# Layer 1's feed-forward with seven block products per hidden tile instead of eight, on one core

## The chip, the core and the metric

The kernel runs on one core of one Trainium2 chip. The core has a matrix engine (PE in the profile, TensorE), three elementwise engines (DVE = VectorE, ACT = ScalarE, POOL = GpSimd), DMA queues that are fed by SP (SyncE), an on-chip memory SBUF of 128 partitions, and a small accumulator memory PSUM that the matrix engine writes. The metric is the device time of one execution in microseconds.

## The reference

A two-layer transformer block for 512 latent tokens and 256 context tokens of width 1024. Each layer is attention followed by a SwiGLU feed-forward, both behind a normalisation with a learned shift, scale and gate. Layer 0 treats latents and context, layer 1 (the last) gives only the latents. The part that the change touches is the feed-forward of layer 1, with F = 2816 hidden units:

```python
def _swiglu(h, w_in, w_out):
    gate, up = jnp.split(h @ w_in, 2, axis=-1)
    return (jax.nn.silu(gate) * up) @ w_out
...
x = x + gx2 * _swiglu(_rms(x, norm_ffn_w[l]) * (1.0 + scx2) + shx2, ffn_w_in[l], ffn_w_out[l])
```

Here `h` is 512 x 1024, `w_in` 1024 x 5632 (gate columns, then up columns), `w_out` 2816 x 1024, all float32; `gx2` is one row of 1024 numbers, the gate row.

## The kernel before

**Split products.** The large products are made in float32r. Every float32 operand z is split in two: `hi` is z rounded to float32r by an ACT copy, `lo = z - hi` is a subtraction (DVE or POOL). A product is three matmuls, hi·hi, hi·lo and lo·hi, accumulated in PSUM. `unit` (L322) loads a raw weight tile by DMA into one of two "raw" buffers (`raw_tile`, L101), and splits it; its argument `sub` names who subtracts. `by_pieces` (L314) subtracts by POOL in pieces of 256 columns.

**Operands.** `hT` holds the normalised activations transposed, hi and lo, each 128 x 8 x 512: partition = place within one of eight groups of 128 inputs, then group k, then token.

**The feed-forward** `ffn` (L786). The 2816 hidden units are 22 F-tiles of 128, taken in 11 pairs p. For a pair, gate and up weights come as four raw tiles of 128 x 4 x 256 (two halves of the inputs, 256 hidden units each), the down weights as two tiles of 128 x 1024. For each F-tile, `half` (L807) makes gate and up with 8 groups x 3 matmuls each, all 512 tokens at once in layer 1, into one PSUM tile `pgu` (two of these exist, tag "sc"). Then ACT makes silu(gate) (L841), DVE multiplies by up (L843), and `split` makes the hidden tile's hi and lo (L444, L445). The down product then sums over the F-tiles at hand (two; the last four together) for each of 4 token tiles x 2 halves of the output columns in one of four PSUM banks (`dps`, L868 to L870), and `residual` (L435) multiplies by the gate row `g` (L438) and adds into the token tile `xs[t]` (L439), both on DVE. `g` is made by `gate_row` (L248), which goes through DRAM, in the first pair. The first pair of layer 1 is made in two halves of 256 tokens, since the second half's `hT` is ready later. When the last sums of a half row are done, that half row goes to `out`.

**Ahead of it**, layer 1's attention runs over 8 heads. `in_proj1` (L607) loads four weight units for a head (two groups of inputs each, 128 x 768), split by ACT and, all four, by POOL in pieces. The output projection has eight weight units (`units1`, L1114): those with k = 4 to 7 live in the pool "w1u", which afterwards holds gate and up weights. Unit k = 6 has a raw tile of its own (`late_raw`), the others use the two shared raw buffers.

**What sets the order.** The framework schedules each engine's instructions from a simulated timeline, by program order as priority and by when operands are ready there; each engine then works off its list strictly in that order. A buffer of a ring is written again only after its last reader. A pool that is opened on the place of a closed one waits tile by tile for what lay there.

## Time and profile before

| | |
|---|---|
| median of three runs | 1791.71 us (1789.78 to 1797.6) |
| profiled execution | 1790.93 us, its span 1789.1 us |
| PE busy | 1718.5 us, 96% of the span |
| DVE, ACT, POOL busy | 998.0, 807.0, 608.9 us |
| mean granted PE clock | 0.992 of full |
| feed-forward of layer 1 | from 1411.2 us to the end |

PE's busy time holds overlaps of pipelined matmuls, so it doesn't show how densely PE works; the distance in time between starts of neighbouring matmuls does. "PEld" is the weight load of a matmul, which overlaps the one before. In a table of stages the columns are the stretch, its length, the busy time of each engine with the number of instructions in brackets, the granted clock, the DMA engines' busy share, and GB/s. In a timeline the columns are start, duration, engine, line, operation, output<-inputs and shape, and in square brackets how long the engine had been idle and who ended that.

### The profile page before, as it was taken

The numbers are of one execution on the slowest core, as the hardware profiler recorded it, in microseconds if no ns is written. First come the engines' busy times: TensorE is split into PE (matmuls) and PEld (weight loads), VectorE is DVE, ScalarE is ACT, GpSimd is POOL, SyncE is SP. The second block draws the span as 40 slices with busy tenths as digits, with TensorE's granted clock in tenths as the row PEclk, the third lists the DMA queues.
The fourth block names the chain that finished last, engine by engine and source line by source line (L and its number), as shares of the span: only waits on it lengthen the run. The fifth ranks groups of instructions, "written<-read, shape, count | busy, mean of one in ns | idle before, by whom it ended". The sixth has DMA issues, their size and how long they took to land.

```text
span 1789.1 us, 26195 instructions
## 1 busy us (share of the span) xinstructions
PE 1718.5 (96%) x9958; PEld 1455.3 (81%) x9958; DVE 998.0 (56%) x1738; ACT 807.0 (45%) x1713; POOL 608.9 (34%) x880
## 2 busy tenths in 40 slices
PE   6999999989999999999999999999988999999998
PEld 4987776767888888888888889999976888888887
DVE  4776465435265555555552756666564565656653
ACT  6666555434264344343332566666653432232230
POOL 2753333321054344222231767777752200000000
PEclk8999999999999999999999999999999999999999
DMA  9112233203552334343331211111121243233231
GB/s 318 53 42 88 79 100 124 72 31 112 161 156 80 100 104 152 122 130 126 109 97 45 85 36 47 44 49 41 57 71 60 69 131 96 71 114 98 71 111 54
DMA packets 152478, 165.64 MB, mean 93 GB/s; under 512 B 16481, under 2 KB 139937, under 8 KB 152353
## 3 DMA queue, kind: packets, MB, share of 16 engines
q1 hardware_dynamic: 152000, 163.77, 29.5%
q8 instruction: 78, 1.28, 0.3%
q14 instruction: 48, 0.39, 0.1%
q10 hardware_dynamic: 352, 0.21, 0.0%
HBM read 159.73 MB, written 4.22 MB: 92 GB/s over the span
## 4 chain that ended last, share of the span: by engine, by line
PE 71%; issue 6%; POOL 6%; ACT 4%; DVE 4%; DMA 4%; SPq 1%; ACTq 0%; POOLq 0%; DVEq 0%
PE pgu L813 13%; PE pu L813 8%; PE pg L813 8%; PE dps L868 5%; PE dps L869 5%; PE dps L870 5%; PE inps L431 3%; PE inps L432 3%; PE inps L433 3%; POOL wil L320 2%; PE av L582 2%; PE sc L537 2%; PE ops L752 2%; PE ops L754 2%; PE ops L753 2%
## 5 line engine op out<-in xcount | busy, mean ns | idle before, releaser
L438 DVE TENSOR_TENSOR dps<-dps,g 128x512 f32<-128x512 f32 x200 | 136.0, 695 | 105.2 <-PE dps L870 96.8
L868 PE MATMUL dps<-wdh,hdh 128*128 128x512 f32 x440 | 175.9, 401 | 1.7 <-DVE x L439 1.0
L869 PE MATMUL dps<-wdl,hdh 128*128 128x512 f32 x440 | 174.4, 396 | 0.0
L870 PE MATMUL dps<-wdh,hdl 128*128 128x512 f32 x440 | 167.8, 396 | 0.0
L431 PE MATMUL inps<-wih,hT 128*128 128x384 f32 x384 | 132.9, 346 | 1.8 <-ACT qkv L629 1.1
L439 DVE TENSOR_TENSOR x<-x,dps 128x512 f32<-128x512 f32 x200 | 131.9, 681 | 2.6
L433 PE MATMUL inps<-wih,hT 128*128 128x384 f32 x384 | 130.8, 341 | 0.0
L432 PE MATMUL inps<-wil,hT 128*128 128x384 f32 x384 | 130.5, 340 | 0.0
L813 PE MATMUL pu<-hT,wuh 128*128 128x512 f32 x352 | 129.4, 391 | 0.5 <-DVE x L439 0.5
L813 PE MATMUL pg<-hT,wgh 128*128 128x512 f32 x352 | 129.8, 392 | 0.0
L212 ACT ACTIVATE modw<-modw,cols 128x256 f32<-128x256 f32 x192 | 82.1, 498 | 82.5 <-DMA modw<-in_mod_w_dram 78.2
L813 PE MATMUL pgu<-hT,wuh 128*128 128x512 f32 (+1 forms) x384 | 113.3, 376 | 0.0
L813 PE MATMUL pgu<-hT,wgh 128*128 128x512 f32 (+1 forms) x384 | 112.3, 376 | 0.4 <-DVE hT L308 0.4
L868 PEld LDWEIGHTS dps<-wdh,hdh 128*128 128x128 f32 x440 | 82.7, 188 | 23.6 <-issue 3.3
L813 PE MATMUL pg<-hTc,wgh 128*128 128x256 f32 x352 | 99.0, 285 | 2.7 <-ACT hTc L307 2.4
L333 ACT CAST wgh<-wgr 128x1024 fp32r<-128x1024 f32 x44 | 46.0, 1049 | 121.9 <-PE pgu L813 71.2
L813 PE MATMUL pu<-hTc,wuh 128*128 128x256 f32 x352 | 98.4, 284 | 0.0
L870 PEld LDWEIGHTS dps<-wdh,hdl 128*128 128x128 f32 x440 | 82.3, 188 | 19.6
L869 PEld LDWEIGHTS dps<-wdl,hdh 128*128 128x128 f32 x440 | 82.8, 188 | 17.8
L334 DVE TENSOR_TENSOR wgl<-wgr,wgh 128x1024 fp32r<-128x1024 f32 x44 | 55.0, 1254 | 75.3 <-ACT wgh L333 75.3
L320 POOL TENSOR_TENSOR wil<-wir,wih 128x256 fp32r<-128x256 f32 x96 | 76.4, 824 | 56.3 <-ACT wih L333 56.0
L334 DVE TENSOR_TENSOR wul<-wur,wuh 128x1024 fp32r<-128x1024 f32 x44 | 58.1, 1321 | 61.8 <-ACT wuh L333 61.8
(263 smaller groups left out, 4626.1 us busy)
## 6 DMA issues: line engine op xcount, KB each, us to landing
modw<-in_mod_w_dram SPq DMA_DIRECT2D x96, 512.0 KB, 4.5
wgr<-in_ffn_w_in_dram SPq DMA_DIRECT2D x44, 512.0 KB, 3.5
wur<-in_ffn_w_in_dram SPq DMA_DIRECT2D x44, 512.0 KB, 3.5
wdr<-in_ffn_w_out_dram SPq DMA_DIRECT2D x44, 512.0 KB, 3.5
wir<-in_od_w_in_dram SPq DMA_DIRECT2D x96, 128.0 KB, 2.3
x<-in_x_dram SPq DMA_DIRECT2D x8, 512.0 KB, 6.7
wir<-in_ev_w_in_dram SPq DMA_DIRECT2D x16, 256.0 KB, 2.9
wor<-in_ev_w_out_dram SPq DMA_DIRECT2D x8, 512.0 KB, 3.9
```

Source lines behind the costliest of these rows:

```text
L212: nc.scalar.activation(pr[:, k], w[:, k], AF.Copy, scale=cols[:, kk:kk + 1])
L320: nc.gpsimd.tensor_sub(lo[c], raw[c], hi[c])
L334: (sub or nc.vector.tensor_sub)(lo, raw, f32(hi))
L431: nc.tensor.matmul(ps, hs[0][:, k, :], a, start=k == 0, stop=False)
L432: nc.tensor.matmul(ps, hs[0][:, k, :], b, start=False, stop=False)
L433: nc.tensor.matmul(ps, hs[1][:, k, :], a, start=False, stop=k == KT - 1)
L438: nc.vector.tensor_mul(tmp, ps, g[:, n * 512:(n + 1) * 512])
L439: eng.tensor_add(xt[:, n * 512:(n + 1) * 512], xt[:, n * 512:(n + 1) * 512], tmp)
L813: nc.tensor.matmul(ps[:, s0:s1], a, cols_T(b, s0, s1)[:, k, :], start=k == 0 and q == 0, stop=k == KT - 1 and q == 2)
L868: nc.tensor.matmul(ps, hh, a, start=j == 0, stop=False)
L869: nc.tensor.matmul(ps, hh, b, start=False, stop=False)
L870: nc.tensor.matmul(ps, hl, a, start=False, stop=j == nj - 1)
```

## The change

Layer 1 no longer calls `ffn` but a new function, `ffn_by_blocks`; layer 0 keeps `ffn`. The first pair of F-tiles is made as before (in blocks, `plain_pair`). For each of the other 20 F-tiles, gate and up together are seen as a product of 2 x 2 blocks: weight rows gate and up, the inputs in two halves of 512, the tokens in two halves of 256. Eight block products would be needed in the plain way; here seven are made (Strassen's scheme in Winograd's form), each of 4 groups x 3 matmuls with 256 tokens.

- Weight sums, per F-tile: with a11, a12 the input halves of gate and a21, a22 those of up, r1 = a21+a22, r2 = r1-a11, a11-a21 and a12-r2, on POOL (`combine`), each 128 x 512. Seven weight blocks are split: ACT rounds, POOL subtracts for two of them, DVE for five. They live in a ring of nine (`wb`).
- Activation sums, once: `context` makes four sums t1 to t4 of `hT`'s quarters (128 x 4 x 256 each; three chains on DVE, one on POOL, in two shared raw buffers and two of the four "wr" buffers) and splits them.
- Sums of products, per F-tile: one ACT copy and seven DVE additions of 128 x 256 in PSUM, ahead of silu.
- Weights come as 128 x 8 x 128 tiles, one for gate and one for up per F-tile, in a ring of four ("wr").
- Down sums: x is written to `out` after the first pair, `xs[t]` becomes an accumulator that ACT fills from the first sums, and later sums are added by DVE without the gate row. After the sums of F-tiles 16 and 17 the gate row is made, x is read back, and `xs = xs * g + x`. The sums of the last four F-tiles go through `residual` as before.
- In the input projection, heads 0 and 1 have two of their four weight units subtracted by DVE instead of POOL. In the output projection, unit k = 6 uses the shared raw buffers. The pool "w1u" is closed ahead of the feed-forward, and pools for the blocks and the down weights are opened.

```diff
--- before.py
+++ after.py
@@ -613,7 +613,7 @@
                     yield raw[:, :, j * P:(j + 1) * P], od_w_in[
                         0, u * 256:(u + 1) * 256, j * D + h * P:j * D + (h + 1) * P].rearrange(
                         "(j p) n -> p j n", p=P)
-            ws.append(unit(wh, views, [P, 2, 384], 5, "wi", by_pieces))
+            ws.append(unit(wh, views, [P, 2, 384], 5, "wi", None if h < 2 and u % 2 else by_pieces))
         kT = st.tile([P, 2, TOK], F32R, name="kT", tag="kT")
         vv = st.tile([P, NT, P], F32, name="vv", tag="vv")
         qs = {}
@@ -872,6 +872,168 @@
                     if p == NF // 2 - 1:
                         done(t, n)
             wo, hid = [], []
+
+    def ffn_by_blocks(l, xs, new_blocks, new_down, fp, rooms, done):
+
+        half = KT // 2
+        cols = SEQ // 2
+        wf = ffn_w_in[l]
+        hh = [fp.tile([P, SEQ], F32R, name=f"hd{z}", tag=f"hd{z}", bufs=4) for z in "hl"]
+
+        def load(f, up):
+            raw = fp.tile([P, KT, P], F32, name="wr", tag="wr", bufs=4)
+            c0 = up * FFN + f * P
+            nc.sync.dma_start(raw, wf[:, c0:c0 + P].rearrange("(j p) n -> p j n", p=P))
+            return raw[:, :half], raw[:, half:]
+
+        def block():
+            return [new_blocks(z) for z in "hl"]
+
+        def halves(raw, eng=nc.vector):
+            hi, lo = block()
+            nc.scalar.copy(hi, raw)
+            eng.tensor_sub(lo, raw, f32(hi))
+            return hi, lo
+
+        def combine(a, b, op):
+            r = fp.tile([P, half, P], F32, name="ws", tag="ws", bufs=4)
+            nc.gpsimd.tensor_tensor(r, a, b, op)
+            return r
+
+        def down(f):
+            raw = raw_tile([P, D], "wdr")
+            hi, lo = new_down("h"), new_down("l")
+            nc.sync.dma_start(raw, ffn_w_out[l, f * P:(f + 1) * P, :])
+            nc.scalar.copy(hi, raw)
+            nc.vector.tensor_sub(lo, raw, f32(hi))
+            return hi, lo
+
+        def product(out, a, b, start=True, stop=True):
+            for k in range(half):
+                for x, y, q in ((a[0], b[0], 0), (a[0], b[1], 1), (a[1], b[0], 2)):
+                    nc.tensor.matmul(out, x[:, k, :], y[:, k, :], start=start and k == 0 and q == 0,
+                                     stop=stop and k == half - 1 and q == 2)
+
+        b11, b12, b21, b22 = ([hT[z][0][:, k * half:(k + 1) * half, c * cols:(c + 1) * cols] for z in range(2)]
+                              for k in range(2) for c in range(2))
+
+        def places():
+            ps = p_sc.tile([P, 1024], F32, name="pgu", tag="sc")
+            return ps, ps.rearrange("p (r c) -> p r c", c=cols)
+
+        def hidden(ps, first=None):
+            pu, pg = ps[:, :SEQ], ps[:, SEQ:]
+            sg = fp.tile([P, SEQ], F32, name="sg", tag="sg", bufs=1)
+            nc.scalar.activation(sg, pg, AF.Silu)
+            nc.vector.tensor_mul(pu, sg, pu)
+            hi, lo = first or [fp.tile([P, SEQ], F32R, name=f"hd{z}", tag=f"hd{z}", bufs=4) for z in "hl"]
+            nc.scalar.copy(hi, pu)
+            nc.vector.tensor_sub(lo, pu, f32(hi))
+            return hi, lo
+
+        def plain_pair():
+            ws, ps = [], []
+            for f in range(2):
+                raws = [load(f, up) for up in range(2)]
+                ws.append([[halves(r) for r in raw] for raw in raws])
+                ps.append(places())
+            for c, bs in enumerate(((b11, b21), (b12, b22))):
+                for f in range(2):
+                    for up in range(2):
+                        for k in range(2):
+                            product(ps[f][1][:, (0 if up else 2) + c], ws[f][up][k], bs[k], k == 0, k == 1)
+            return [hidden(ps[0][0], hh), hidden(ps[1][0])]
+
+        def context():
+            t1, t2, t3 = (room() for room in rooms)
+            sub, add = ALU.subtract, ALU.add
+            f1, f2 = (raw_tile([P, half, cols], f"tf{i}") for i in range(2))
+            f3, f4 = (fp.tile([P, half, cols], F32, name=f"tf{i}", tag="wr", bufs=4) for i in (2, 3))
+            for eng, t, terms in ((nc.vector, f1, ((b12[0], b11[0], sub), (None, b12[1], add), (None, b11[1], sub))),
+                                  (nc.gpsimd, f3, ((b22[0], b12[0], sub), (None, b22[1], add), (None, b12[1], sub))),
+                                  (nc.vector, f2, ((b22[0], f1, sub), (None, b22[1], add))),
+                                  (nc.vector, f4, ((b21[0], f2, sub), (None, b21[1], add)))):
+                for a, b, op in terms:
+                    eng.tensor_tensor(t, t if a is None else f32(a), f32(b), op)
+            for t, raw in ((t2, f2), (t1, f1), (t3, f3), (b12, f4)):
+                nc.scalar.copy(t[0], raw)
+                nc.vector.tensor_sub(t[1], raw, f32(t[0]))
+            return t1, t2, t3, b12
+
+        def by_blocks(f):
+            (a11, a12), (a21, a22) = (load(f, up) for up in range(2))
+            w11 = halves(a11)
+            r1 = combine(a21, a22, ALU.add)
+            r2 = combine(r1, a11, ALU.subtract)
+            s2 = halves(r2, nc.gpsimd)
+            s1 = halves(r1, nc.gpsimd)
+            s3 = halves(combine(a11, a21, ALU.subtract))
+            w12 = halves(a12)
+            s4 = halves(combine(a12, r2, ALU.subtract))
+            w22 = halves(a22)
+            ps, z = places()
+            e, b, a, c = (z[:, i] for i in range(4))
+            q, u, v, w = (fp.tile([P, cols], F32, name=n, tag=n, bufs=1) for n in "quvw")
+            product(a, w11, b11)
+            nc.scalar.copy(q, a)
+            product(b, s2, t2)
+            nc.vector.tensor_add(u, b, q)
+            product(c, s1, t1)
+            nc.vector.tensor_add(v, c, u)
+            product(e, s3, t3)
+            nc.vector.tensor_add(b, e, v)
+            nc.vector.tensor_add(w, e, u)
+            product(a, w12, b21)
+            nc.vector.tensor_add(a, a, q)
+            product(c, s4, b22)
+            nc.vector.tensor_add(c, c, v)
+            product(e, w22, t4)
+            nc.vector.tensor_add(e, e, w)
+            return hidden(ps)
+
+        def sums(hid, wd, last, first):
+            for t in range(NTX):
+                for n in range(2):
+                    turn["sum"] = (turn["sum"] + 1) % 4
+                    ps = p_1.tile([P, 512], F32, name="dps", tag=("acc0", "tr0", "acc1", "tr1")[turn["sum"]])
+                    for j in range(len(hid)):
+                        x, y = (z[:, t * P:(t + 1) * P] for z in hid[j])
+                        a, b = (z[:, n * 512:(n + 1) * 512] for z in wd[j])
+                        nc.tensor.matmul(ps, x, a, start=j == 0, stop=False)
+                        nc.tensor.matmul(ps, x, b, start=False, stop=False)
+                        nc.tensor.matmul(ps, y, a, start=False, stop=j == len(hid) - 1)
+                    acc = xs[t][:, n * 512:(n + 1) * 512]
+                    if first:
+                        nc.scalar.copy(acc, ps)
+                    elif last:
+                        residual(xs[t], ps, g, n)
+                        done(t, n)
+                    else:
+                        nc.vector.tensor_add(acc, acc, ps)
+
+        g = None
+        hid, wd = [], []
+        for f in range(0, NF, 2):
+            if f == 0:
+                hid.extend(plain_pair())
+                t1, t2, t3, t4 = context()
+                for t in range(NTX):
+                    nc.sync.dma_start(out[0, t * P:(t + 1) * P, :], xs[t])
+            else:
+                hid.extend([by_blocks(f), by_blocks(f + 1)])
+            wd.extend([down(f), down(f + 1)])
+            if f == NF - 4:
+                continue
+            if f == NF - 6:
+                g = gate_row(l, 5, 0, fp)
+            sums(hid, wd, f == NF - 2, f == 0)
+            if f == NF - 6:
+                for t in range(NTX):
+                    xr = raw_tile([P, D], "xr")
+                    nc.sync.dma_start(xr, out[0, t * P:(t + 1) * P, :])
+                    nc.vector.tensor_mul(xs[t], xs[t], g)
+                    nc.vector.tensor_add(xs[t], xs[t], xr)
+            hid, wd = [], []
 
     class Pairs:
 
@@ -1108,15 +1270,12 @@
     def out_pool(k):
         return woe.pool if k < 2 else in_ctx_room if k < 4 else w1[0].pool
 
-    def late_raw(shape, name):
-        return opa.pool.tile(shape, F32, name=name, tag="wor", bufs=1)
-
     def units1():
         subs = (by_pieces, by_pieces, by_pieces, by_pieces, None, nc.gpsimd.tensor_sub, None, nc.gpsimd.tensor_sub)
         for k in range(KT):
             def views(raw, k=k):
                 yield raw, od_w_out[0, k * P:(k + 1) * P, :]
-            yield unit(out_pool(k), views, [P, D], 2 if k < 2 else 4, "wo", subs[k], late_raw if k == 6 else raw_tile)
+            yield unit(out_pool(k), views, [P, D], 2 if k < 2 else 4, "wo", subs[k])
 
     oproj = OutProj(1, units1(), o_t, xs)
 
@@ -1171,14 +1330,27 @@
     states[0].close()
     at.close()
     woe.close()
-    w1.append(Pool("w1d", "right"))
+    w1.pop().close()
+    blocks = Pool("w1b", "right")
+    downs = Pool("w1d", "right")
     fp = Pool("ffn1")
-    ffn(1, xs, NTX, w1, fp.pool,
-        lambda t, n: nc.sync.dma_start(out[0, t * P:(t + 1) * P, n * 512:(n + 1) * 512],
-                                       xs[t][:, n * 512:(n + 1) * 512]))
+
+    def new_room(j):
+        if j < 2:
+            if not rooms:
+                rooms.extend(ctx_room([P, 2, KT // 2, SEQ // 2], F32R, "tc"))
+            return rooms[j][:, 0], rooms[j][:, 1]
+        return [keep.tile([P, KT // 2, SEQ // 2], F32R, name=f"t3{z}", tag="xo", bufs=6) for z in "hl"]
+
+    rooms = []
+    ffn_by_blocks(1, xs, lambda z: blocks.pool.tile([P, KT // 2, P], F32R, name="wb" + z, tag="wb" + z, bufs=9),
+                  lambda z: downs.pool.tile([P, D], F32R, name="wd" + z, tag="wd" + z, bufs=4), fp.pool,
+                  [lambda j=j: new_room(j) for j in range(3)],
+                  lambda t, n: nc.sync.dma_start(out[0, t * P:(t + 1) * P, n * 512:(n + 1) * 512],
+                                                 xs[t][:, n * 512:(n + 1) * 512]))
     fp.close()
-    w1[1].close()
-    w1[0].close()
+    downs.close()
+    blocks.close()
 
 
 def _constants():
```

## The prediction

> **What bounds the kernel now.** I read the stage table of the feed-forward first, then the groups of instructions in its even part, then single instructions. The stage table of the kernel before (PE's last block of the first pair ends at 1436.4, the last sum at 1784.6):
>
> ```profile
> core 0: us, PE busy (x) PEld busy (x) DVE busy (x) ACT busy (x) POOL busy (x), PEclk, DMA share, GB/s
> 1411.17:1436.40 25.23, 24.78 (x210) 24.36 (x208) 14.71 (x23) 15.01 (x24) 2.92 (x3) 1.00 0.45 142
> 1439.95:1761.90 321.95, 321.95 (x1381) 258.93 (x1380) 184.74 (x241) 80.58 (x96) 0.00 (x0) 1.00 0.31 93
> 1761.90:1784.61 22.71, 22.71 (x97) 17.91 (x96) 10.52 (x16) 1.19 (x2) 0.00 (x0) 1.00 0.20 78
> ...
> 1527.60:1729.00 201.40, 201.40 (x865) 161.99 (x864) 118.83 (x156) 50.80 (x60) 0.00 (x0) 1.00 0.32 94
> ```
>
> From 1440 on PE has no gap: 864 matmuls of 512 tokens in 201.40 us are one every 0.2331 us, at full clock, and a pair of F-tiles (96 for gate and up, 48 for down) takes 33.6. DVE works 59% of that stretch, ACT 25%, POOL and most of the DMA not at all. So here the number of columns that PE streams sets the time, and fewer columns shorten it until another engine or a late operand takes over. What follows prices both.
>
> **PE's part.** Plain: 48 matmuls of 512 tokens per F-tile. By blocks: 7 x 4 x 3 = 84 of 256, each with a weight load of its own. The old first pair has just that form:
>
> ```profile
> 1425.38:1436.12 10.74, 10.74 (x95) 10.74 (x93) 0.50 (x1) 0.60 (x1) 1.00 0.46 149
> L813 PEld LDWEIGHTS pgu<-hT,wuh x384: 187/187/192, 1417.0 to 1761.3; 128*128 128x128 f32 x192
> ```
>
> Of the 93 loads one was under way at the start: 92 matmuls in 10.74 us, 0.1167 each, so that the loads of 0.188 overlap and cost nothing. Saved per F-tile: 48 x 0.2331 - 84 x 0.1167 = 11.19 - 9.80 = 1.39 us, for 20 F-tiles **27.7**. The new pitch can't be much under half of the old (0.1155: 29.8 saved), and at 0.1245, with transposes in between, 14.6 would be left. The first pair keeps its columns, the down sums theirs, and the last sums (22.7 us, then 4.5 to the end) are the same: 0 each.
>
> **What the other engines get.** Means of one, from the even stretch and, for POOL and the 256-wide PSUM operation, from the whole run:
>
> ```profile
> L439 DVE TENSOR_TENSOR x<-x,dps 128x512 f32<-128x512 f32 x64 | 41.6, 680 | 0.3
> L334 DVE TENSOR_TENSOR wgl<-wgr,wgh 128x1024 fp32r<-128x1024 f32 x16 | 19.6, 1226 | 21.8 <-ACT wgh L333 21.8
> L843 DVE TENSOR_TENSOR pgu<-sg,pgu 128x512 f32<-128x512 f32 x16 | 11.1, 693 | 18.7 <-ACT sg L841 18.7
> L445 DVE TENSOR_TENSOR hdl<-pgu,hdh 128x512 fp32r<-128x512 f32 x16 | 10.9, 682 | 0.0
> L333 ACT CAST wgh<-wgr 128x1024 fp32r<-128x1024 f32 x16 | 16.8, 1050 | 63.3 <-PE pgu L813 63.3
> L444 ACT CAST hdh<-pgu 128x512 fp32r<-128x512 f32 x16 | 9.4, 584 | 6.1 <-DVE pgu L843 6.1
> L587 DVE TENSOR_TENSOR o<-av,o 128x256 f32<-128x256 f32 x24 | 10.1, 421 | 31.3 <-PE av L582 31.0
> L213 POOL TENSOR_TENSOR modw<-modw 128x512 f32<-128x512 f32 x48 | 62.1, 1294 | 83.5 <-ACT modw L212 83.5
> L334 POOL TENSOR_TENSOR wol<-wor,woh 128x1024 fp32r<-128x1024 f32 x10 | 24.5, 2456 | 18.6 <-ACT woh L333 18.6
> ```
>
> Per pair of F-tiles, against PE's new 2 x 9.80 + 48 x 0.2331 = 30.8 us:
> - DVE: per F-tile five splits of 0.68, one down split of 1.23, seven additions of 0.42, silu's product and the hidden split 1.38, together 9.0; and eight plain additions of 0.68 per pair where there were sixteen operations (the product with g is gone): 23.4.
> - POOL: 12 operations of 1.29: 15.5.
> - ACT: per F-tile eight casts or copies of 0.58 at most, a down cast of 1.05, silu and hidden cast 1.2: 13.9.
> - DMA: the same bytes per F-tile in 8% less time; a 512 KB tile lands in 3.5 us (last fence) of the 15.4 that an F-tile takes, three of them, and two F-tiles of raw weights are in flight.
>
> None reaches 30.8 by itself. But DVE and POOL now work on SBUF together, which the old feed-forward of layer 1 never did. Layer 0's shows what that costs:
>
> ```profile
> 520.79 1.29 POOL L213 TENSOR_TENSOR modw<-modw 128x512 f32<-128x512 f32 x1
> 521.45 1.73 DVE L334 TENSOR_TENSOR wul<-wur,wuh 128x1024 fp32r<-128x1024 f32 x1
> ...
> 628.30 1.62 DVE L334 TENSOR_TENSOR wul<-wur,wuh 128x1024 fp32r<-128x1024 f32 x1
> 628.80 1.72 POOL L215 TENSOR_TENSOR ma<-modw 128x256 f32<-128x256 f32 x1
> ...
> L334 DVE TENSOR_TENSOR wul<-wur,wuh 128x1024 fp32r<-128x1024 f32 x22 | 31.2, 1417 | 28.1 <-ACT wuh L333 28.1
> 418.00:960.00 542.00, 538.33 (x2932) 455.36 (x2931) 284.28 (x384) 217.60 (x393) 169.64 (x166) 1.00 0.38 120
> ```
>
> A split that starts 0.63 before POOL's operation ends takes 0.50 longer; whoever starts second waits. With POOL busy 31% of the time a split took 0.19 more (1.417 against 1.226). With POOL at 15.5 of 30.8, 50%, I take 0.31 for each of DVE's twelve two-input SBUF operations per pair: 3.7, so DVE at 27.1 of 30.8. The least is 0, the most a whole POOL operation each, 15.5, which makes 38.9. I take PE to stay the bound, with **3** us lost in all where an addition that PE waits for stands behind a blocked split (bounds 0 and, as a rival, below): the product sequence gives each of those additions two products, 2.8 us, before its place is written again.
>
> The Trainium skill, page "SBUF — State Buffer", section "Who interferes with whom", says that a DVE instruction with two SBUF inputs and a POOL instruction that reads SBUF exclude each other, and the second fully blocks until the first is done. The rows above agree (1.73 against 1.23). By its words alone every collision costs up to a whole instruction, which is the 38.9 above and the third rival below; by the mean row it is 27.1.
>
> **The start.** The four activation sums need all of `hT`:
>
> ```profile
> 1423.99 1.29 DVE L308 TENSOR_TENSOR hT<-nhc,hT 128x512 fp32r<-128x512 f32 x2 [1.03 <-ACT hT L307]
> ...
> 1437.06 0.50 PE L868 MATMUL dps<-wdh,hdh 128*128 128x512 f32 x1 [0.67 <-ACT hdh L444]
> ```
>
> From 1425.3 DVE makes f1 (3 operations of 1.23) and f2 (2), then t2's split (1.05 + 1.23): 1433.7 if nothing interferes, before PE is through the first pair and one product more, 1436.4 + 1.4 = 1437.8. But POOL makes f3 then, three operations of 2.46: if each f1 operation waits for one, t2 is there at 1441.1, 3.3 late. Behind it on DVE stand the other three splits, f4, two hidden tiles and the first weight splits, and the first down weights wait for the raw buffers that f1 and f2 hold: t1's split at 1442.3, then 3.5 + 1.05 + 1.23 to 1448. PE has the two new F-tiles (19.6 us) to do meanwhile, in pieces. Some 2 us more, and a stretch at half clock if PE idles (1.7: half of the 3.3 that such a stretch costs in the last fence's rows). I take **7**; at best 0, at worst 25, if DVE (22.1 us of work) and POOL (15.1) go strictly in turn from 1425.3 and PE gets no work until 1462.5. Writing x to `out` is 2 MB on SP's queue in a stretch with DMA at 0.45; weights are two tiles ahead, and the gate row's transfers leave this place: 0, within those bounds.
>
> **The turn to x.** Between the sums of F-tiles 16 and 17 and the last sums, PE has 11.2 + 4 x 9.80 = 50.4 us. DVE has 4 x 9.0 + 5.4, and eight operations of 1.23 for x g + x: 51.2, with 32 waits of 0.31 61. The ring of nine blocks brings 4.4 of it forward, and the last x is wanted only in the last sums. I take **4** (0 to 12).
>
> **The input projection.** Head 1's weights are late today:
>
> ```profile
> 1037.00:1042.00 5.00, 2.34 (x14) 1.58 (x12) 2.36 (x5) 2.71 (x5) 4.76 (x9) 0.97 0.55 156
> 1042.00:1049.00 7.00, 6.37 (x29) 5.93 (x30) 1.00 (x3) 2.87 (x7) 6.57 (x12) 0.53 0.40 113
> L320 POOL TENSOR_TENSOR wil<-wir,wih 128x256 fp32r<-128x256 f32 x90 | 72.2, 830 | 4.0 <-ACT wih L333 3.8
> L334 DVE TENSOR_TENSOR wil<-wir,wih 128x768 fp32r<-128x768 f32 x4 | 3.8, 946 | 0.0
> wdr<-in_ffn_w_out_dram SPq DMA_DIRECT2D x44, 512.0 KB, 3.5
> ```
>
> POOL is full, PE idles 3.3 us and then runs 7 us at half clock, 3.3 more. Two of four units go from three POOL pieces of 0.83 to one DVE operation of 0.95 on an engine that is busy 3.4 us of these 12: 5 us less on POOL per head. All of 6.6 could go, or nothing, if the load behind is late instead; I take 4. Unit k = 6 of the output projection now uses a buffer that is free earlier; PE has gaps there, I take 1 (0 to 2). Together a gain of **5**.
>
> The Trainium skill, page "TensorE: Matmul & The Clock Gate", section "What's actually happening", gives half the clock after an idle window of about 3.4 us. The row at 0.53 comes behind an idle of 3.3 us that was broken by single matmuls, so the rule's window is measured by activity here. By the rule a start with short gaps alone would keep the clock, and the start's term would be 5.3 instead of 7.
>
> **Sum**, against the profiled execution's 1790.93 us (span 1789.1 and 1.8 around it): 1790.9 - 27.7 - 5 + 3 + 7 + 4 = 1772.2. The median is 0.8 above that execution: **1773**.
>
> **The rivals.**
> 1. *Everything hides*: losses near 2, the input projection gives 6. 1790.9 - 27.7 - 6 + 2 = 1759. For it: no engine is over 90% by the sum. Against it: three stretches in which DVE has as much to do as PE.
> 2. *Start and turn eat it*: 18 and 10 there, 3 in between, the input projection gives 2: 1790.9 - 27.7 - 2 + 31 = 1792, no change. For it: the chain behind f1 is serial, and the ring's plain blocks are only freed as the first pair ends. Against it: PE has two F-tiles' products to fill in with.
> 3. *DVE becomes the bound, by the lock* (slower). DVE takes over when a two-input operation waits more than (30.8 - 23.4) / 12 = 0.62, and the time of before is passed when a pair takes 33.0, at a wait of 0.80. At 1.0 a pair takes 35.4, 4.6 over PE for ten pairs: 1790.9 - 27.7 - 5 + 11 + 46 = 1815. For it: the two 1.7 rows; DVE's list is in order, so a blocked split holds up the additions that PE waits for. Against it: the mean of 0.19 in layer 0.
>
> That the saving isn't there at all I leave out: the matmul counts stand in the code, and the 0.1167 in a row.
>
> **How the numbers follow.** A measurement of this kernel tells 0.5%, 9 us, from no change: 1782.8 and 1800.7. The forecast (1762 to 1785) gets 0.60, rival 1 0.10, rival 2 0.15, rival 3 0.13, and 0.02 goes to something slower that I don't name. Faster: forecast, rival 1 and a little of rival 2's spread, 0.72; the same: most of rival 2, 0.13; slower 0.15. The likeliest own range is 1762 to 1785; the range to hold the time 8 times in 10 goes from the best bound (1758) past rival 2 to 1796.
>
> **What would show it.** Right: a pair of F-tiles in the even stretch takes 30.8 us with PE without gaps; DVE's 128 x 512 splits average 0.8 to 1.0 and DVE stays under 90%; PE has its gaps behind 1436 and behind the sums of F-tiles 16 and 17, and no half clock at 1042. Wrong: a pair that takes over 31.5, PE waiting for an addition or a split on DVE all along (rival 3), gaps of over 15 us in those two places (rival 2), or matmuls of 256 tokens further apart than 0.12.

## The result and the profile after

The changed kernel takes **1860.21 us** (median of 4 runs, 1855.1 to 1867.1) where the kernel before takes 1791.07 beside it: a ratio of 1.038, 95% interval 1.034 to 1.043. Forecast were 1773 and a range to 1796, so the forecast missed by 87 us and on the wrong side.

Head of the page of the changed kernel, then its table of stretches (columns as in the prediction): a pair of F-tiles in the even part, three stretches from the start of the blocks, and the turn to x.

```profile
span 1865.3 us, 28324 instructions
...
PE 1725.4 (92%) x10678; PEld 1490.9 (80%) x10678; DVE 1080.9 (58%) x1885; ACT 864.2 (46%) x1849; POOL 790.5 (42%) x991
```

```profile
1597.24:1634.58 37.34, 32.30 (x216) 29.09 (x216) 24.11 (x40) 13.55 (x23) 17.12 (x12) 1.00 0.28 85
...
1420.00:1440.00 20.00, 20.00 (x164) 20.00 (x163) 18.50 (x20) 8.43 (x17) 11.14 (x6) 0.94 0.02 9
1440.00:1460.00 20.00, 11.43 (x66) 9.88 (x66) 17.86 (x16) 13.50 (x20) 10.17 (x7) 0.83 0.69 203
1460.00:1480.00 20.00, 15.46 (x79) 13.02 (x78) 18.18 (x16) 10.90 (x19) 16.55 (x11) 0.83 0.55 160
1733.00:1837.00 104.00, 90.34 (x577) 80.75 (x577) 66.27 (x102) 30.12 (x50) 34.31 (x23) 0.95 0.22 66
```

A pair takes 37.3 us. Forecast were 30.8, and 33.6 was the old value. No engine is near full there: DVE works 24.1, POOL 17.1, ACT 13.6, and PE itself 32.3. Ten pairs at 6.5 us over the forecast are 65 of the 87 us. PE is not short of work but kept waiting, in the even part for the same two operations each time (waits of PE from 1410 to the end: total, times, longest; the third row lies at the start and behind it):

```profile
PE pgu L914 <- DVE v L982: 33.6, 20, 1.9
PE pgu L914 <- DVE pgu L987: 13.8, 20, 1.4
PE dps L1002 <- ACT hdh L930: 11.1, 3, 6.0
```

20 times each is once per F-tile: the addition that makes `v`, and `a += q`. One such wait, on PE's, DVE's and POOL's timelines of the changed kernel (start, duration, in brackets the idle time before it and its releaser):

```profile
1602.89 1.50 DVE L895 TENSOR_TENSOR wbl<-ws,wbh 128x512 fp32r<-128x512 f32 x1 [0.16 <-ACT wbh L894]
1604.31 0.68 DVE L928 TENSOR_TENSOR pgu<-sg,pgu 128x512 f32<-128x512 f32 x1
1604.91 0.41 DVE L982 TENSOR_TENSOR v<-pgu,u 128x256 f32<-128x256 f32 x1
...
1603.38 0.28 PE L914 MATMUL pgu<-tc,wbl 128*128 128x256 f32 x1
1605.37 0.39 PE L914 MATMUL pgu<-t3h,wbh 128*128 128x256 f32 x1 [1.71 <-DVE v L982]
1605.60 0.28 PE L914 MATMUL pgu<-t3l,wbh 128*128 128x256 f32 x1
...
1602.55 1.29 POOL L900 TENSOR_TENSOR ws<-wr 128x512 f32<-128x512 f32 x1
```

The matmul at 1605.37 is the first of the product `e` (s3 by t3). `v` is c + u: it reads nothing of `e`, and `c` lies in the other PSUM bank. Still the matmul waits for it. So what seems to be tracked is not the block of 256 columns but the whole tile `pgu`, 128 x 1024 in two banks: every product waits until the operation on the product before it is done. That is theory T1 below.

Of the 1.71 us, some 0.8 is the lock of the prediction's third rival: the split starts 0.34 after POOL's sum L900 has begun, and takes 1.50 where 0.68 is usual. The Trainium skill, page "SBUF — State Buffer", section "Who interferes with whom", says that the second one blocks until the first is done. The rows agree: POOL's sum ends at 1603.84, the split 0.55 later. That the lock makes DVE late, whatever PE waits for, is theory T2. A further 0.6 is the silu product L928 of the tile before.

### The profile page after: what moved, and what is told of

Read it like the earlier page. It is cut to its first block, busy times and chain, and to the rows that moved or that the text cites. A ratio compares the mean times of both kernels' runs of the same rounds, so it can differ in the third digit from the quotient of the medians.

```text
span 1865.3 us, 28324 instructions
## 1 busy us (share of the span) xinstructions
PE 1725.4 (92%) x10678; PEld 1490.9 (80%) x10678; DVE 1080.9 (58%) x1885; ACT 864.2 (46%) x1849; POOL 790.5 (42%) x991
## 5 line engine op out<-in xcount | busy, mean ns | idle before, releaser
L914 PE MATMUL pgu<-hT,wbh 128*128 128x256 f32 x768 | 143.4, 286 | 18.5 <-DVE pgu L987 13.8
L914 PEld LDWEIGHTS pgu<-hT,wbh 128*128 128x128 f32 x768 | 120.2, 190 | 28.1 <-DVE pgu L987 18.0
L438 DVE TENSOR_TENSOR dps<-dps,g 128x512 f32<-128x512 f32 x128 | 87.4, 695 | 77.4 <-PE dps L870 59.1
L895 POOL TENSOR_TENSOR wbl<-ws,wbh 128x512 fp32r<-128x512 f32 x40 | 58.5, 1471 | 149.1 <-ACT wbh L894 147.9
L914 PE MATMUL pgu<-hT,wbl 128*128 128x256 f32 x384 | 108.1, 281 | 0.9 <-DVE wbl L895 0.9
L869 PE MATMUL dps<-wdl,hdh 128*128 128x512 f32 x264 | 104.5, 396 | 0.0
L870 PE MATMUL dps<-wdh,hdl 128*128 128x512 f32 x264 | 101.8, 396 | 0.0
L213 POOL TENSOR_TENSOR modw<-modw 128x512 f32<-128x512 f32 x48 | 62.1, 1294 | 85.4 <-ACT modw L212 85.4
L894 ACT CAST wbh<-ws 128x512 fp32r<-128x512 f32 x80 | 49.5, 621 | 81.3 <-PE pgu L914 78.0
L551 ACT ACTIVATE Pt<-sc,nm 128x256 f32<-128x256 f32 (+3 forms) x96 | 68.0, 712 | 38.1 <-DVE nm L547 14.6
```

The lines of the kernel that those rows point to most:

```text
L438: nc.vector.tensor_mul(tmp, ps, g[:, n * 512:(n + 1) * 512])
L869: nc.tensor.matmul(ps, hh, b, start=False, stop=False)
L870: nc.tensor.matmul(ps, hl, a, start=False, stop=j == nj - 1)
L895: eng.tensor_sub(lo, raw, f32(hi))
L914: nc.tensor.matmul(out, x[:, k, :], y[:, k, :], start=start and k == 0 and q == 0, stop=stop and k == half - 1 and q == 2)
```

## The experiments

Times are medians of device us; "before" ran beside each. From the second group on, *the base* is the kernel of the first experiment.

**1. One-bank tiles.**

```
-            ps = p_sc.tile([P, 1024], F32, name="pgu", tag="sc")
-            return ps, ps.rearrange("p (r c) -> p r c", c=cols)
+            ps = [p_gu.tile([P, SEQ], F32, name=name, tag=name) for name in ("pu", "pg")]
+            return ps, [z[:, i * cols:(i + 1) * cols] for z in ps for i in range(2)]
...
+            product(e, w22, t4)
+            nc.vector.tensor_add(e, e, w)
             product(c, s4, b22)
             nc.vector.tensor_add(c, c, v)
-            product(e, w22, t4)
-            nc.vector.tensor_add(e, e, w)
```

The new tiles come from a PSUM pool of their own, opened where the old pool lay.

> Edit: the changed kernel, with up and gate of an F-tile in two PSUM tiles of one bank each instead of one tile of two banks, and the last two products in the order e, c, so that the seven products write up's and gate's tiles in turn. Theory T1 (each product waits for the elementwise operation that read the product before it in the same two-bank tile, so DVE's latency is PE's): the waits of PE for v (L982) and for a+=q (L987) lose their cause; a pair of F-tiles falls from 37.3 us to 31 to 33, the time from 1860 to 1800 to 1815. Theory T2 (the SBUF lock between DVE and POOL makes DVE late, whatever tile PE waits for): the splits stay at 1.14 and 0.73 us, a pair stays above 36 and the time above 1845.

Measured: **1801.9 us**, ratio to before 1.0048 (1.0031 to 1.0066), 58 less than the changed kernel. Two pairs of the base in the table of stretches, and all of PE's waits from 1523 to 1709:

```profile
1573.85:1636.41 62.56, 61.96 (x434) 57.39 (x433) 52.50 (x77) 26.69 (x45) 37.25 (x24) 1.00 0.35 102
```

```profile
PE pu L915 <- DVE u L981: 1.2, 2, 0.6
```

A pair takes 31.28 us, PE is busy 61.96 of 62.56, and the waits for `v` and `a += q` are gone from the even part. DVE's work per pair did not fall (26.3 against 24.1): the lock is there as before, and costs PE next to nothing.

**2. POOL's part left out.** Two-bank tile as in the changed kernel.

```
-            r1 = combine(a21, a22, ALU.add)
-            r2 = combine(r1, a11, ALU.subtract)
-            s2 = halves(r2, nc.gpsimd)
-            s1 = halves(r1, nc.gpsimd)
-            s3 = halves(combine(a11, a21, ALU.subtract))
-            s4 = halves(combine(a12, r2, ALU.subtract))
+            s2, s1, s3, s4 = copies(a22), copies(a21), halves(a21), halves(a12)
```

`copies` makes both halves of a block by ACT, so ACT has two copies more per F-tile.

> Edit: the changed kernel without any work of POOL in the products: the five sums of weight blocks are left out (s1 to s4 are taken from single blocks, so the output is another), and the low halves of s1 and s2 are copies by ACT. T1: the stall on v loses only the part that the blocked split before it made (about 0.8 of 1.7 us), the one on a+=q stays; a pair takes 34.5 to 36 us, the time is 1835 to 1850. T2: DVE's splits fall to 0.68, a pair falls to 31 to 32, the time to 1795 to 1810.

Measured: 1844.1 us (1.0289, 1.0273 to 1.0305), 16 less. Five pairs, and the waits of PE in them:

```profile
1517.01:1693.94 176.93, 161.15 (x1080) 145.18 (x1080) 110.19 (x191) 78.33 (x131) 0.00 (x0) 1.00 0.30 90
```

```profile
PE pgu L920 <- DVE v L986: 8.8, 10, 0.9
PE pgu L920 <- DVE pgu L991: 6.5, 10, 0.8
```

With POOL at 0.00 a pair still takes 35.4 us. The wait for `v` fell from 1.8 to 0.9 per F-tile, that for `a += q` not at all. These are T1's numbers, not T2's: the lock was a part of the delay, not its cause.

**3. Both.** The edits of 1 and 2 together.

> Edit: both of the above at once (sums of weight blocks left out, output another). T1 and T2: a pair takes what PE's matmuls take, 30.8 us, the time is 1790 to 1805; what is then left above 1773 lies in the start, the turn and the half-clock stretches. If a pair stays above 32, a third cause is at work in the even part.

Measured: 1794.7 us (1.002, 1.0009 to 1.0031). Five pairs:

```profile
1501.34:1659.80 158.46, 156.25 (x1089) 144.45 (x1088) 104.95 (x192) 74.51 (x130) 0.00 (x0) 1.00 0.34 100
```

A pair takes 31.7, no less than the base with POOL at work, though ACT has more to do here (14.9 a pair against 13.3). What POOL costs the base, 5 to 7 us by the ratios and the medians, lies outside the even part.

**4. One bank or the order?** The first experiment made two edits; here is one of them each, on the changed kernel: one-bank tiles in the old order, and the new order in the old tile.

> Edit to the changed kernel: one-bank PSUM tiles, with the products in the old order (a, b, c, e, a, c, e). T1: only the product c that follows directly on a still waits for an operation on its own bank (a+=q), about 1.0 us per F-tile where nothing else fills it; the time is 1805 to 1818, so the tile's size carries most of the 58 us. If the order carries it: above 1840.

> Edit to the changed kernel: the last two products in the order e, c, in the old two-bank tile. T1: each product still waits for the operation on the product before it: 1850 to 1866, no change against the changed kernel. If the order carries it: 1805 to 1820.

Measured: **1808.1** and **1866.4 us** (1.0091, 1.0077 to 1.0105, and 1.0414, 1.0398 to 1.043). PE's waits in five pairs of the second are those of the changed kernel:

```profile
PE pgu L914 <- DVE v L982: 18.1, 10, 1.9
PE pgu L914 <- DVE pgu L987: 6.5, 10, 0.8
```

The tile's size carries 52 us and the order alone nothing; with one-bank tiles the order is worth another 6. What PE still waits for in five pairs of the one-bank kernel in the old order:

```profile
PE pg L915 <- DVE v L983: 1.8, 3, 0.6
PE dps L1003 <- ACT hdh L931: 1.5, 2, 0.9
```

The time is as expected, but the wait that was named for it, on `a += q`, is not in the list; in the products from 1583 to 1590 sums of the down product run between `a` and `c`. What is left is `v`: it reads `c`, and the next product in that tile, `a`, waits for it, though in other columns. So a tile of one bank is still counted as a whole. T1 stands; how the 6 us come about is shown only in part.

**5. The two side edits**, alone on the kernel before: head 0's and 1's odd units, and unit k = 6.

> Edit: the kernel before with the two side edits alone: head 0's and 1's odd units split by one DVE operation, and unit k = 6 of the output projection through the common raw buffers. The forecast's term: 5 us faster, 1786. Rival: the input projection gains about 2 (half clock for 3.4 us instead of 6.8), but the output projection ends 4.8 later, as in the trace of after; no change or up to 4 us slower, 1790 to 1795.

Measured: 1789.9 us, ratio 0.9982 (0.9972 to 0.9991): 3.2 us gained, 1.6 to 5.0. The half clock behind 1042 stays: the granted clock from 1042 to 1049 is 0.51 there and 0.53 before, though PE works 3.63 of the five us ahead of it instead of 2.34. The output projection's last matmul runs at 1411.07 there against 1410.93 before, so the rival's late output projection is not the work of these edits. (The profiled executions of both kernels took the same time, 1790.97 and 1790.93 us, so they don't show where the gain lies.)

**6. The start.** The base still lies 29 us above the forecast. Its SP queue and that queue's waits behind the output projection:

```profile
1390.17 18.98 SPq L1022 DMA_DIRECT2D out_dram<-x  x2
1409.25 4.61 SPq L887 DMA_DIRECT2D wr<-in_ffn_w_in_dram  x4
1417.05 0.36 SPq L1022 DMA_DIRECT2D out_dram<-x  x1
1441.90 0.34 SPq L907 DMA_DIRECT2D wdr<-in_ffn_w_out_dram  x1
1442.34 4.54 SPq L887 DMA_DIRECT2D wr<-in_ffn_w_in_dram  x3
...
SPq L907 <- DVE tc L961: 24.5, 1, 24.5
SPq L1022 <- POOL x L440: 18.2, 1, 18.2
```

The first down load waits 24.5 us for the buffer that f1 holds, and F-tile 2's weights stand behind it; ahead of the first weights stand the stores of x. That looked like the cause. Four edits of the base: f1 to f4 moved to the down ring and the down loads ahead; the stores of x issued by ACT's queue; x g + x moved into the last sums; all three together, with the activation sums on DVE alone. Their main lines:

```
-            f1, f2 = (raw_tile([P, half, cols], f"tf{i}") for i in range(2))
-            f3, f4 = (fp.tile([P, half, cols], F32, name=f"tf{i}", tag="wr", bufs=4) for i in (2, 3))
+            f1, f2, f3, f4 = (f32(new_down(z)).rearrange("p (k c) -> p k c", c=cols) for z in "hlhl")
...
-                    nc.sync.dma_start(out[0, t * P:(t + 1) * P, :], xs[t])
+                    nc.scalar.dma_start(out[0, t * P:(t + 1) * P, :], xs[t])
...
-                        residual(xs[t], ps, g, n)
+                        nc.vector.tensor_add(ps, acc, ps)
+                        nc.vector.tensor_mul(ps, ps, g[:, c])
+                        nc.vector.tensor_add(acc, ps, xr[t][:, c])
```

> Edit to the one-bank kernel (1802 us, call it the base): the first two down tiles are loaded ahead of the activation sums, and the four sums f1 to f4 stand in four slots of the down ring instead of the raw buffers and weight buffers. Theory Q (SP's queue is in order: the first down load waits 24.5 us for f1's raw buffer, and the weight loads of F-tile 2 stand behind it, so DMA moves nothing from 1420 to 1440): the loads of F-tile 2 are issued by 1426, PE's gaps of 5.6 us behind 1443 and most of the half clock there go, 6 to 12 us: 1790 to 1796. Theory L (the lock between DVE and POOL in f1 to f3 is what makes the start late): t2 still comes at 1441 and later, the gap stays in another place, 0 to 3 us: 1799 to 1802.

> Edit to the base: the four stores of x to DRAM are issued by ACT's queue instead of SP's. Theory Q: the first four weight loads no longer stand behind a store that waits for the output projection's x (18.2 us), they are issued by 1395 to 1405 instead of 1409.3, and the first block matmul runs at 1412 instead of 1417.5: 3 to 6 us, 1796 to 1799. Rival: the loads' own room (the buffers of the output projection) is free no earlier than that, no change, 1802.

> Edit to the base: the eight operations of x g + x behind the sums of F-tiles 16 and 17 are left out; the last sums take three operations each ((acc + dps) g + x) instead of two, and x comes back into weight buffers that are free by then. Theory: DVE has 9.8 us less to do in 1722 to 1742, and the last four down loads no longer stand in SP's queue behind the loads of x; PE's gaps and half clock from 1733 to 1782 shrink by 6 to 10 us, the last operation adds 0.7: 1793 to 1797. Rival: PE waits there for the down weights and hidden tiles anyway, 0 to 3 us: 1799 to 1802.

> Edit to the base: the three edits above together, and all four activation sums on DVE alone (no POOL beside it). If the three causes are separate, the gains add: 1775 to 1786, faster than before by 0.4 to 1.0%. If they share one cover (DVE's work at the start), 1788 to 1795, no change against before.

Measured: 1805.1, 1802.4, 1799.2 and 1798.1 us (ratios to before 1.0066, 1.0054, 1.0033, 1.0029). None of the four can be told from the base's 1.0048 (1.0031 to 1.0066) by its interval. The last has a median 3.8 us lower, where 16 to 27 were expected for separate causes, and lies outside the other case's range too. Theory Q, that the order in SP's queue makes the start late, falls. The queue did what the edit meant, and PE waits for another thing (the kernel with the early down loads: SP's queue, waits of PE; then one stretch of the kernel with all four):

```profile
1423.49 5.93 SPq L887 DMA_DIRECT2D wr<-in_ffn_w_in_dram  x4
...
PE dps L1002 <- ACT hdh L931: 13.1, 3, 9.4
```

```profile
1440.00:1460.00 20.00, 13.02 (x82) 11.12 (x80) 20.00 (x17) 9.75 (x16) 13.52 (x7) 0.91 0.33 103
```

F-tile 2's weights are issued at 1423.5 instead of 1442.3, and now the hidden tiles are 9.4 late. In the second row DVE is busy 20.00 of 20.00 us: earlier loads only bring more work to a full engine. (Busy here holds what an operation waits for the lock: the additions of f1 to f4 take 1.2 to 2.3 us each there.) That is theory D: from 1420 to 1470 DVE's own work bounds the start. Two runs test it: the activation sums left out, and a second plain pair to cover them (with the down ring, ACT's queue and DVE alone as in the last of the four). A third leaves out the eight operations and four loads of the turn.

```
-                for a, b, op in terms:
-                    eng.tensor_tensor(t, t if a is None else f32(a), f32(b), op)
...
+            elif f == 2:
+                hid.extend(plain_pair(f))
+                t1, t2, t3, t4 = context()
...
-                    nc.vector.tensor_mul(xs[t], xs[t], g)
-                    nc.vector.tensor_add(xs[t], xs[t], xr)
```

> Edit to the base (one-bank kernel, 1802 us): the eleven additions that make f1 to f4 are left out (the casts and splits of t1 to t4 stay and take single activation blocks, so the output is another); their buffers are not taken either. Theory D (from 1420 to 1470 DVE has more work than PE, and that is what bounds the start, whatever comes first in a queue): DVE loses 8 operations of 1.2 to 2.3 us, the lock with POOL goes, PE's gaps and half clock behind 1443 shrink from 16 us to 5: 1789 to 1793. Rival: the hidden tiles, down splits and first weight sums come late by themselves: 1796 to 1801.

> Edit to the base: the eight operations x g + x and the four loads of x are left out (output another). It prices the whole turn. If PE's gaps from 1733 to 1782 come from them, 1788 to 1793; if the gap ahead of the last sums (the last hidden tile, whose partial sums PE has already made) stays, as with the turn put in the last sums (1799), 1796 to 1799.

> Edit to the base: the second pair of F-tiles is plain too, so that the activation sums (all on DVE, in the down ring, stores of x on ACT's queue) have 33 us more of PE's work beside them. PE does 2.8 us more. Theory D: the start's 16 us of gaps and half clock fall to 3 or less: 1802 + 2.8 - 13 = 1792, range 1789 to 1795. Rival (PE waits for something other than DVE's work at the change from plain to blocks): the gaps only move by a pair, 1801 to 1806.

Measured: **1789.3**, 1794.9 and **1787.7 us** (0.9982, 0.9972 to 0.9992; 1.0006, 0.9996 to 1.0016; 0.9969, 0.9954 to 0.9985). The eleven additions of f1 to f4 cost 12.6 us, as theory D has it, and a second plain pair hides them: 14 less for 2.8 more of PE's work, a little more than theory D's range had. Leaving the sums out also frees the buffers that they hold, but moving them out of these buffers gained nothing above. Whether it is DVE's full list or the serial chain of the sums that PE waits for, the two runs don't separate. The stretch from 1440 in the base, without the additions, and with two plain pairs:

```profile
1440.00:1460.00 20.00, 13.24 (x74) 11.51 (x73) 16.64 (x17) 11.85 (x19) 9.35 (x6) 0.83 0.67 200
```

```profile
1440.00:1460.00 20.00, 19.73 (x134) 17.92 (x133) 13.30 (x14) 12.66 (x22) 14.24 (x10) 1.00 0.42 131
```

```profile
1440.00:1460.00 20.00, 20.00 (x143) 18.64 (x142) 15.51 (x15) 7.58 (x12) 12.19 (x6) 1.00 0.31 87
```

PE goes from 13.24 to 19.73 and to 20.00, and the clock from 0.83 to 1.00 with it. Without its eight operations and four loads the turn gives back 7.0 us, between the ranges of the two cases, so neither is confirmed.

**7. The turn again**, on the kernel with two plain pairs: first x g + x ahead of the last sums, by POOL and DVE; then both operations by POOL, held behind POOL's last weight split (`at[True]`). The second edit:

```
-                    nc.gpsimd.tensor_mul(xs[t], xs[t], g)
-                    nc.vector.tensor_add(xs[t], xs[t], xr)
+                    with tc.issue_after(at[True].ins):
+                        nc.gpsimd.tensor_mul(xs[t], xs[t], g)
+                        nc.gpsimd.tensor_add(xs[t], xs[t], xr)
```

> Edit to the kernel with two plain pairs: x g + x moves from behind the sums of F-tiles 16 and 17 to ahead of the last sums, the four products by POOL, the four additions by DVE, x in weight buffers. Forecast: the turn's 12 us of gaps and half clock fall to 6: 6 less than the kernel with two plain pairs, 1783 to 1789, at or a little below the kernel before.

> Edit to the kernel with two plain pairs and the moved turn (1786): both operations of x g + x by POOL, placed behind POOL's last weight split, so that no weight of the last F-tiles and no sum that PE waits for stands behind them. If they are what is left of the turn: PE's gaps between 1715 and 1750 (5 us and 1.7 at half clock) go: 1780 to 1783. If it is the last hidden tile's own chain (gap of 2.6 ahead of the last sums): 1784 to 1787.

Measured: 1786.0 us (0.9960, 0.9947 to 0.9972), not to be told from 0.9969 without the move; and **1779.8 us (0.9935, 0.9922 to 0.9948)**, 11 us faster than the kernel before (9 to 14 by the interval). The second edit changes both the place and the engine of the additions, and no run separates the two. The trace favours the place: in the first edit POOL's four products run from 1715 to 1726 and its next weight splits stand behind them, in the second they start at 1730.7, behind the last split. Of the last kernel: the start, six even pairs, and all of PE's longer waits from 1415 to the end.

```profile
1440.00:1460.00 20.00, 20.00 (x146) 18.76 (x145) 16.06 (x15) 8.15 (x13) 12.40 (x6) 1.00 0.33 96
...
1527.29:1715.09 187.80, 186.01 (x1299) 172.36 (x1298) 157.01 (x230) 80.11 (x133) 111.71 (x72) 1.00 0.35 105
```

```profile
PE pu L917 <- DVE u L982: 2.4, 4, 0.6
PE dps L1004 <- ACT hdh L933: 2.1, 1, 2.1
PE dps L1004 <- DVE x L440: 1.3, 1, 1.3
```

A pair takes 31.3 us, and no wait is longer than 2.1 us.

## Why the prediction was wrong

**The step that failed** is the even part's term, +3 us, and in it the sentence "the product sequence gives each of those additions two products, 2.8 us, before its place is written again". It counted the slack by *place*, by 256 columns. The tile is what counts, and then the slack is nothing: each product waits for the reader of the one just before. The term is 65 us instead of 3 (37.3 against 30.8, ten pairs). Of 6.5 us per pair, 4.9 are the two waits (18.1 and 6.5 for five pairs); the other 1.5 is PE's busy time, 32.3 instead of 30.8. Most of that comes with the waits too: in the wait shown above matmuls start at 1603.38, 1605.37 and 1605.60, so against a pitch of 0.117 the stop costs 2.0 us where the wait counts 1.71. Counted so from start to start, the stops of the five pairs (a shorter one for `c += v` among them) come to 6.2 us per pair.

The trace of before had it already. In its even stretch PE makes gate first and up behind it, both in one tile `pgu`, and silu needs gate alone (PE's timeline, gate's last matmul and up's last; then ACT's):

```profile
1579.74 0.40 PE L813 MATMUL pgu<-hT,wgl 128*128 128x512 f32 x1
...
1588.13 0.39 PE L813 MATMUL pgu<-hT,wul 128*128 128x512 f32 x1
...
1588.62 0.60 ACT L841 ACTIVATE sg<-pgu 128x512 f32<-128x512 f32 x1 [9.97 <-PE pgu L813]
```

Gate is complete at 1580.1, silu starts at 1588.6, right behind up's last matmul. It cost nothing there, since PE had other work, and so no group or wait of PE pointed at it. The change turned the same rule into PE's own wait.

The Trainium skill, page "PSUM — Partial Sum Buffer", section "PSUM bank collisions raise a hardware error", says, in its simple version, that PSUM is to be guarded by bank and not by address: an engine may not touch a bank's partitions while another does, even in other columns. By that rule the wait between `c` and `a`, in one bank, has to be there, and only the one across banks can go. The runs agree as far as they go: one-bank tiles took 52 us away, and the wait of `a` for `v` within a bank was still there with them. What happens when two engines do touch one bank at once no run here tried.

**PE's part, 27.7: right, nearly to the size.** Once PE is not kept waiting, a pair takes 31.3 us instead of 33.6, that is 2.3 less of the forecast 2.8. **The other engines' work: right** within about 10% in the changed kernel: DVE 24.1 (forecast 23.4, and 27.1 with the lock), POOL 17.1 (15.5), ACT 13.6 (13.9). In the base, where the pairs follow each other faster, POOL's is 18.6, 20% over.

**The third rival named the sign and not the cause.** It said that PE waiting for an addition on DVE all along would show the lock. Exactly that was in the trace, and the lock made only half of one of the two waits. A sign that two causes share tells neither.

**The start, 7: too small, by the right mechanism.** The activation sums cost 12.6. The text gave DVE 22.1 us of work there and saw f1 collide with f3, and that collision is in the trace: f1's three additions take 8.0 us, 1.2 each being usual, and t2's split ends at 1447.1 instead of 1441.1. But the text let PE's next F-tiles fill the time, and these wait for the same full list of DVE: PE's longest wait in the changed kernel, 6.0 us, is there, for a hidden tile. "Weights are two tiles ahead" was wrong too (0.02 of DMA from 1420 to 1440), though mending that gained nothing.

**The turn, 4: measured 7.0. The side edits, 5: measured 3.2** (1.6 to 5.0); the half clock at 1042 that they were to shorten stayed.

**What is left.** Base, less the sums, less the turn: 1801.9 - 12.6 - 7.0 = 1782.3, if the two add up, which no run tested. The forecast without its own start and turn is 1762. Of the 20 between, the side edits are 2 and the even pairs 2 (31.28 against 30.8 + 0.3, ten times). The rest I can only place, and not all of it. The last matmul of the output projection, in before, in the changed kernel and in the fastest one:

```profile
1410.93 0.40 PE L754 MATMUL ops<-woc,hT 128*128 128x512 f32 x1
```

```profile
1415.53 0.40 PE L754 MATMUL ops<-woc,hT 128*128 128x512 f32 x1
```

```profile
1412.36 0.40 PE L755 MATMUL ops<-woc,hT 128*128 128x512 f32 x1
```

From there to the end of the span it is 378.2, 449.8 and 363.8 us; the base takes 387.0. Without the activation sums it is 374.9 and without the turn 379.5, so both prices, 12.1 and 7.5 here, come out again by this count. What comes ahead of it ends between 1411.3 (experiment 3) and 1419.1 (the first edit of experiment 7, against 1411.8 without it) in kernels whose edits lie behind it. With one profile of each I can't tell whether that is the kernel or the execution; why is open. The first block product starts 2.5 us after that matmul in the changed kernel, 0.24 before, and in the base and the fastest kernel the last sums wait for the last hidden tile (2.6 and 2.1). The fastest kernel's 363.8 is close to what the forecast gave this stage (378.2 - 27.7 + 3 + 7 + 4 = 364.5), but by other terms: it has a second plain pair and another place for the turn. That the two agree is luck.

## What to carry to other kernels

Slack in PSUM is counted by the tile that the waits are kept for (two banks here, one bank in the mended kernels), not by the columns that an operation touches: give results that different engines read in turn a tile of one bank each, and alternate the banks. Before trusting a slack, look in the trace of before for an operation that waits for a part of a tile which it doesn't read. And where one engine is full, moving its operands forward may gain nothing, as here; leave work out once to learn its price, then look for a neighbour stage that can cover it.

## What the hardware showed that I had not expected

With one-bank tiles the SBUF lock between DVE and POOL costs the even part next to nothing. DVE's work is longer for it, 26.3 us a pair with POOL's 18.6 beside it and 21.0 without any, but all of PE's waits in five pairs of the base are 1.2 us.

And the granted clock can fall behind a pause of under 2 us. In the changed kernel PE waits 1.92 us for `v` until 1732.99, with none longer from 1710 on, and right behind it the clock is at half:

```profile
1731.00:1733.00 2.00, 0.09 (x2) 0.01 (x1) 2.00 (x4) 0.97 (x2) 1.92 (x2) 1.00 0.00 0
1733.00:1735.00 2.00, 2.00 (x9) 2.00 (x10) 1.28 (x2) 0.23 (x1) 1.82 (x2) 0.52 0.02 7
```

The same happens at 1756 and 1773, behind waits of 1.95 and 1.91 (0.62 and 0.63 in the four us that follow). From 1523 to 1709 ten such waits of up to 1.9 us left the clock at 1.00. So the length of the pause alone does not decide it.
